# A state-space mixer's chunks in another column order, and sixteen small matmuls in another place

## The chip, the core and the metric

The kernel runs on one core of a Trainium2 chip. The metric is the device time of one execution in microseconds. PE is the matmul engine (PEld its weight loads), ACT the scalar engine, DVE the vector engine, POOL the general-purpose engine, SP the engine that issues most DMAs. Each engine executes its own list of instructions strictly in order; semaphores make one engine wait for another.

## What is computed

A transformer-like block on 512 tokens of width 1024, in fp32: a norm, an input projection, then two mixers side by side (a state-space mixer and a dilated attention), gates and an output projection, a feed-forward part with a three-tap convolution, a last gated branch and a norm. The change lies in the state-space mixer and beside the projections for the attention:

```python
z = rms_norm(x) @ w_in            # s_in (512), q, k, v (768 each), gates (2048)
# state-space mixer, 32 groups of 16 channels, 64 complex states per group
bu = einsum('blgh,gph->blgp', s_in, bbar)        # complex
s[l] = a * s[l-1] + bu[l]                        # along the sequence
y = gelu(einsum(s, c) + d * s_in); y = y * sigmoid(y @ glu_w + glu_b)
# attention: rotary on q and k, 12 heads of 64, three dilation patterns
```

## The kernel before

**Tokens and tiles.** Token 4c + r is held at column (or partition) c of residue r; r runs over 4, c over the 128 chunks of four tokens. "By residue" means tiles of 128 tokens with the same r, "by tile" means 128 tokens that follow each other (32 chunks with all four residues).

**Products.** Each fp32 weight chunk of 128 x 1024 is loaded by SP into wr (L127), copied by ACT to a high part wh (L128), and the rest is formed by DVE as the low part wl (L129). Each of the three rings has three buffers. One product is three matmuls of 512 columns (`mm3`, L149 to L151): high-high, high-low, low-high. PE's stream is thus almost wholly such triples, and each chunk of weights needs its ACT and its DVE step in time. `proj_tok` (L307) makes one 512-column projection of all tokens, one PSUM tile (pa) per residue; its evacuation runs ahead of other work in priority.

**Background work.** The state-space mixer is a Python generator, `g_ssm` (L424). After every second chunk `tick` (L275) lets it issue steps until a budget is used up; each `yield` names the cost that its author put down for the step. A scheduler turns the program order and the priorities (`ahead`) into one list of instructions per engine when the program is built, by its own estimate of times; nothing is reordered when it runs.

**The recurrence.** U holds the input by chunk (a transpose by PE, an evacuation by ACT, L656 to L660). es (L667) are the contributions of each chunk to the state, one set for the real and one for the imaginary part (i), for 16 pairs of groups (q). ACT writes them shifted by one chunk into E (L668), 128 columns per q. DVE then runs the recurrence over the chunks in steps of `cstep` (L680): four products into scr (the real and imaginary part, each times two factors), one sum into both parts, and two sums into one part each, all at L413, the line of the helper `tt`. The steps are, in order:

- three long steps over 32 columns per q, within blocks of four chunks (L695);
- three middle steps over 8 columns (L698), seven short steps over one column (L701), three middle steps over 7 columns (L704), on the last column of each block;
- three long steps over 31 columns (L707), which hand the block's start on to its other columns.

With 16 q, a long product has 512 (or 496) columns, and the sum into both parts 1024 (or 992). In the kernel before, chunk c stands in column c, so the long steps touch every fourth column and the middle steps every sixteenth. After them, ys (L717 to L719) takes E, U and two factor tensors to the outputs Yg, and yT (L725 to L729) is their transpose, evacuated by ACT.

**The projections for the attention.** After the state-space input come v (heads 4 to 11), then three projections j = 0, 1, 2 of q and k heads. ACT evacuates each residue (L372), DVE applies the rotary factors (L381 to L386, six operations of 64 columns), and PE transposes the result (`to_heads`, L392). These transposes are put on a list, `later`, and issued at the next tick. In PE's list they stand between matmuls of the next projection; the ones of j = 2 stand in the first v product.

**The factors by tile.** The norm's factor y1[0] is held by residue. L852 to L858 turn it into y1[1], by tile: sixteen matmuls of one column each into the PSUM tile yps, and one DVE copy, y1t (L857). Only the evacuation of the last v heads (L365) reads it. `ax_tile` tiles (yps, es, transposes and so on) share three PSUM buffers; a buffer is free again when the tile's last reader has finished.

Of the kernel before, what the change touches and what calls it, by code (L numbers as in the profile page):

```python
# [12 lines left out]
AF = mybir.ActivationFunctionType  # L13
# [8 lines left out]
R = 4  # L22
# [15 lines left out]
A_BUDGET = 3.4  # L38
# [26 lines left out]
def tile_hybrid_block(ctx: ExitStack, tc: tile.TileContext, xT, xtok, pT, W, vecs, consts, ssm, out):  # L65
    nc = tc.nc
    ACT, DVE, POOL, PE = nc.scalar, nc.vector, nc.gpsimd, nc.tensor
# [8 lines left out]
    def slot(i, shape, name, dt=F32):  # L76
        return sb.tile([P] + shape, dt, tag=f"s{i}", name=name)
# [4 lines left out]
    def mm_tile(name):  # L82
        return pm.tile([P, 512], F32, tag="mm", name=name)
# [4 lines left out]
    def t_tile(name):  # L88
        return ring.tile([P, 512], F32, tag="t", name=name, bufs=4)
# [19 lines left out]
    def ahead(offset=AHEAD):  # L109
        return tc.high_priority(offset=offset)  # L110
# [47 lines left out]
    def u_split(u, k, src, gcol, c=slice(0, SEQ)):  # L158
        ACT.activation(u[0][k][:, c], src[:, c], AF.Copy, scale=v1(gcol + k))  # L159
        DVE.scalar_tensor_tensor(u[1][k][:, c], src[:, c], v1(gcol + k), u[0][k][:, c].bitcast(F32), op0=ALU.mult, op1=ALU.subtract)  # L160
# [140 lines left out]
    def residue(a, r):  # L301
        return a[:, r * 128:(r + 1) * 128]
# [4 lines left out]
    def proj_tok(evac, first=False, budget=0.0, hooks=None):  # L307
        wA = WTiles(512)
        pss = [mm_tile(f"pa{r}") for r in range(R)]
        for k in range(KD):  # L310
            if first:
                with ahead():
                    if k:
                        u_split(u, k, x[:, k, :], V_MIX)
            w = wA.next()
            for r in range(R):
                mm3(pss[r], (residue(u[0][k], r), residue(u[1][k], r)), w, k == 0, k == KD - 1)
            if hooks and k in hooks:
                hooks[k]()
            if k % 2 == 1 and k < KD - 1:  # L320
                tick(budget)
        if first:

            with ahead(2 * AHEAD):
                for r in range(R):
                    evac(r, pss[r])
            tick(budget)
            return
        tick(budget)
        with ahead(2 * AHEAD):  # L330
            for r in range(R):
                evac(r, pss[r])
# [36 lines left out]
    def ev_qk(j):  # L369
        def ev(r, ps):  # L370
            t = t_tile("qk")
            ACT.activation(t, ps, AF.Copy, scale=y1[0][:, r:r + 1])  # L372
            th = t.rearrange("p (n d) -> p n d", d=64)
            x1 = th[:, :, 0:8]
            x2 = th[:, :, 8:16]
            cosb = rope[:, r, 0:1, :].to_broadcast([P, 8, 8])
            nsin = rope[:, r, 1:2, :].to_broadcast([P, 8, 8])
            psin = rope[:, r, 2:3, :].to_broadcast([P, 8, 8])
            a = ring.tile([P, 2, 8, 8], F32, tag="ra", name="ra", bufs=2)
            b = ring.tile([P, 2, 8, 8], F32, tag="rb", name="rb", bufs=2)  # L380
            DVE.tensor_tensor(a[:, 0], x1, cosb, op=ALU.mult)  # L381
            DVE.tensor_tensor(a[:, 1], x2, cosb, op=ALU.mult)
            DVE.tensor_tensor(b[:, 0], x2, nsin, op=ALU.mult)
            DVE.tensor_tensor(b[:, 1], x1, psin, op=ALU.mult)
            DVE.tensor_tensor(x1, a[:, 0], b[:, 0], op=ALU.add)
            DVE.tensor_tensor(x2, a[:, 1], b[:, 1], op=ALU.add)  # L386
            later.append(functools.partial(to_heads, r, t))

        def to_heads(r, t):
            pt = ax_tile("qkT")  # L390
            for i in range(4):
                PE.transpose(pt[:, i * 128:(i + 1) * 128], t[:, i * 128:(i + 1) * 128], ident)  # L392
            ptv = pt.rearrange("p (i n) -> p i n", i=4)
            n0 = 0
            if j == 0:

                n0 = 2
                ACT.activation(qk[0][:, 0:2, :].rearrange("p i (t r n) -> p i t r n", t=4, r=R)[:, :, :, r, :],
                               ptv[:, 0:2].rearrange("p i (t n) -> p i t n", t=4), AF.Copy)
            ACT.activation(qk[j][:, n0:4, r * 128:(r + 1) * 128], ptv[:, n0:4], AF.Copy)  # L400
        return ev
# [22 lines left out]
    def g_ssm():  # L424
# [133 lines left out]
        AA = {1: A[1], 2: A[2], 3: A[3], 4: A[4], 8: A8, 12: A12, 16: A16}  # L558
# [53 lines left out]
        for i in range(2):  # L612
            for q4 in range(4):
                ps = ax_tile("g1t")
# [39 lines left out]
        U = slot("U", [NQ, P], "U")  # L654
        for q4 in range(4):
            ps = ax_tile("ut")  # L656
            for q in range(4):
                PE.transpose(ps[:, q * 128:(q + 1) * 128], flat(S, q4 * 4 + q), ident)
            ACT.activation(U[:, q4 * 4:q4 * 4 + 4, :].rearrange("p q c -> p (q c)"), ps, AF.Copy)
            yield 0.15  # L660
        E = slot("x", [2, NQ, P], "E")
        DVE.memset(E[:, :, :, 0:1], 0.0)
        for i in range(2):
            for q4 in range(4):
                ps = ax_tile("es")
                for q in range(4):
                    PE.matmul(ps[:, q * 128:(q + 1) * 128], G1[i][:, q4 * 4 + q, :], U[:, q4 * 4 + q, :], start=True, stop=True)  # L667
                ACT.activation(E[:, i, q4 * 4:q4 * 4 + 4, 1:128], ps.rearrange("p (q c) -> p q c", q=4)[:, :, 0:127], AF.Copy)  # L668
                yield 0.15

        G2 = [slot(f"g{i}", [NQ, 2, R, H], f"G2{i}") for i in range(2)]
# [8 lines left out]
        def cstep(dst, src, a_, n):  # L680

            tv = scr[:, 0:2 * NQ * n].rearrange("p (i q n) -> p i q n", i=2, q=NQ)
            uv = scr[:, 1024:1024 + 2 * NQ * n].rearrange("p (i q n) -> p i q n", i=2, q=NQ)
            arb = a_[0].unsqueeze(2).to_broadcast([P, NQ, n])
            aib = a_[1].unsqueeze(2).to_broadcast([P, NQ, n])
            for i in range(2):
                tt(tv[:, i], src[:, i], arb, ALU.mult)
                tt(uv[:, i], src[:, i], aib, ALU.mult)
            tt(dst, dst, tv, ALU.add)
            tt(dst[:, 0], dst[:, 0], uv[:, 1], ALU.subtract)  # L690
            tt(dst[:, 1], dst[:, 1], uv[:, 0], ALU.add)

        E4 = E.rearrange("p i q (b f) -> p i q b f", f=4)
        E16 = E.rearrange("p i q (s f) -> p i q s f", f=16)
        for i in range(1, 4):  # L695
            cstep(E4[:, :, :, :, i], E4[:, :, :, :, i - 1], AA[1], 32)
            yield 4.77
        for i in range(1, 4):  # L698
            cstep(E16[:, :, :, :, 4 * i + 3], E16[:, :, :, :, 4 * i - 1], AA[4], 8)
            yield 1.53  # L700
        for s in range(1, 8):  # L701
            cstep(E16[:, :, :, s:s + 1, 15], E16[:, :, :, s - 1:s, 15], AA[16], 1)
            yield 0.58
        for i in range(3):  # L704
            cstep(E16[:, :, :, 1:8, 4 * i + 3], E16[:, :, :, 0:7, 15], AA[4 * (i + 1)], 7)
            yield 1.40
        for i in range(3):  # L707
            cstep(E4[:, :, :, 1:32, i], E4[:, :, :, 0:31, 3], AA[i + 1], 31)
            yield 4.64

        Yg = slot("S", [R, 32, H], "Yg")
        for q4 in range(4):
            ps = ax_tile("ys")
            for q in range(4):
                qq = q4 * 4 + q
                o = ps[:, q * 128:(q + 1) * 128]
                PE.matmul(o, U[:, qq, :], flat(T, qq), start=True, stop=False)  # L717
                PE.matmul(o, E[:, 0, qq, :], flat(G2[0], qq), start=False, stop=False)
                PE.matmul(o, E[:, 1, qq, :], flat(G2[1], qq), start=False, stop=True)  # L719
            ACT.activation(  # L720
# [3 lines left out]
        yT = slot("U", [4, SEQ], "yT")  # L724
        for mt in range(4):  # L725
            ps = ax_tile("yt")
            for r in range(R):
                PE.transpose(ps[:, r * 128:(r + 1) * 128], Yg[:, r, mt * 8:(mt + 1) * 8, :].rearrange("p g h -> p (g h)"), ident)
            ACT.activation(yT[:, mt, :], ps, AF.Copy)  # L729
            yield 0.15  # L730
        env["yT"] = yT

# [113 lines left out]
    hooks[R] = factors  # L846
    proj_tok(ev_v12, False, A_BUDGET, hooks)
    rb1 = rstd_bc(y1[0], "n1")
    for j in range(3):
        proj_tok(ev_qk(j), False, A_BUDGET)  # L850

    yps = ax_tile("yps")  # L852
    for t_ in range(4):
# [2 lines left out]
    yt_ = small([4], "y1t")  # L856
    DVE.tensor_copy(yt_, yps[:, 0:4])  # L857
    y1.append(yt_)  # L858
    for m in range(2):
        ps = mm_tile("v0")  # L860
        gemm(ps, KD, u)
        tick(A_BUDGET)
        with ahead():
            ev_v0(m, ps)
# [4 lines left out]
    for m in range(16):  # L869
        ps = mm_tile("gps")  # L870
        gemm(ps, KD, u)
        g = gt[m // 4][:, m % 4, :]
# [5 lines left out]
    yT, bh, bl = env["yT"], env["bh"], env["bl"]  # L878
# [16 lines left out]
    for m in range(4):  # L895
        ps = mm_tile("lps")
# [36 lines left out]
    for m in range(KD):  # L933
        ps = mm_tile("ops")
# [10 lines left out]
    for part in range(2):  # L945
# [28 lines left out]
        for m in range(KD):  # L974
            ps = mm_tile("dps")
# [13 lines left out]
    for m in range(KD):  # L989
        ps = mm_tile("pps")  # L990
# [31 lines left out]
    for m in range(KD - NLAST):  # L1022
        ps = mm_tile("eps")
# [25 lines left out]
    for gi, rs in enumerate(LAST):  # L1049
        c = slice(rs[0] * 128, rs[-1] * 128 + 128)  # L1050
        end = gi == len(LAST) - 1
        for m in tail:
            ps = mm_tile("eps")[:, 0:128 * len(rs)]
# [174 lines left out]
```

## Time and profile before

| | us |
|---|---|
| median of 3 runs | 820.05 (820.04 to 821.41) |
| the profiled execution, its own time | 820.38 |
| its span, first to last instruction | 818.3 |
| PE busy | 801.2 (98%) |
| DVE busy | 508.5 (62%) |
| ACT busy | 346.4 (42%) |
| mean granted TensorE clock | 0.987 |

The span is what the profile's views cover; about 2.1 us lie around it. A busy PE says that it had work, not at which clock. Matmuls overlap, so that rows of 0.39 us follow each other every 0.23 us at the full clock; rows of DVE and ACT overlap by about 0.1 us as well. In the views below, times are in microseconds from the start of the span, except means, which are marked or given in ns.

### The profile page before, as it was taken

Reading aid. Unit: us, or ns where it says so; the run is one execution under the profiler, and the core shown is the slowest. Engines: PE = TensorE matmul, PEld = TensorE weight load, DVE = VectorE, ACT = ScalarE, POOL = GpSimd, SP = SyncE. Lnnn points to the kernel's source line nnn. Section 1 sums busy time; section 2 is a strip of 40 time slices with the busy share of each in tenths; the row PEclk is TensorE's granted clock in tenths of the full one; section 3 lists DMA queues with packets and bytes.
Section 4 is the critical chain, followed back from the end, with each engine's and each line's share of the span. In section 5 each row is a group of like instructions: output and inputs, shape, how many; then the busy total and the mean of one; then the engine's idle time right before and its main releaser. Section 6 shows DMA issues by size and latency. Waiting matters only on the chain.

```text
span 818.3 us, 10848 instructions
## 1 busy us (share of the span) xinstructions
PE 801.2 (98%) x4294; PEld 664.3 (81%) x4294; DVE 508.5 (62%) x944; ACT 346.4 (42%) x543; POOL 10.9 (1%) x10
## 2 busy tenths in 40 slices
PE   9999989799999999999999999999999999999996
PEld 7888868589777788888888888888888888888886
DVE  7963999992354447855776555332565556445586
ACT  6773632335344434344354433222344434335454
POOL 2001000000000000000000000000000000000000
PEclk9999998799999999999999999999999999999999
DMA  7731111122111123442322233223322332233202
GB/s 279 269 99 57 51 53 59 70 82 74 53 52 53 53 78 103 139 153 96 128 98 85 101 103 104 88 92 104 103 94 88 104 103 87 95 103 103 81 23 103
DMA packets 23810, 78.97 MB, mean 97 GB/s; under 512 B 2640, under 2 KB 3024, under 8 KB 23760
## 3 DMA queue, kind: packets, MB, share of 16 engines
q1 hardware_dynamic: 23616, 78.22, 28.2%
q8 instruction: 33, 0.54, 0.3%
q14 instruction: 17, 0.14, 0.1%
q10 hardware_dynamic: 144, 0.07, 0.0%
HBM read 76.18 MB, written 2.10 MB: 96 GB/s over the span
## 4 chain that ended last, share of the span: by engine, by line
PE 86%; DVE 10%; ACT 2%; issue 1%; DMA 0%; DVEq 0%; ACTq 0%
PE pg L151 5%; PE pu L151 5%; PE dps L150 5%; PE dps L151 5%; PE pu L150 5%; PE pu L149 5%; PE pg L150 5%; PE pg L149 5%; PE dps L149 5%; PE gps L149 4%; PE gps L151 4%; PE gps L150 4%; DVE E L413 3%; DVE scr L413 2%; PE pa L150 2%; PE pa L151 2%
## 5 line engine op out<-in xcount | busy, mean ns | idle before, releaser
L128 ACT ACTIVATE wh<-wr 128x1024 fp32r<-128x1024 f32 (+1 forms) x132 | 138.1, 1047 | 297.7 <-issue 61.6
L129 DVE TENSOR_TENSOR wl<-wr,wh 128x1024 fp32r<-128x1024 f32 (+1 forms) x132 | 160.0, 1213 | 68.2 <-ACT wh L128 67.9
L150 PE MATMUL pu<-u2l,wh 128*128 128x512 f32 x176 | 68.5, 389 | 0.0
L149 PE MATMUL pu<-u2h,wh 128*128 128x512 f32 x176 | 68.5, 389 | 0.0
L151 PE MATMUL pg<-u2h,wl 128*128 128x512 f32 x176 | 68.5, 389 | 0.0
L149 PE MATMUL pg<-u2h,wh 128*128 128x512 f32 x176 | 68.5, 389 | 0.0
L150 PE MATMUL pg<-u2l,wh 128*128 128x512 f32 x176 | 68.5, 389 | 0.0
L149 PE MATMUL dps<-ah,wh 128*128 128x512 f32 x176 | 68.5, 389 | 0.0
L150 PE MATMUL dps<-al,wh 128*128 128x512 f32 x176 | 68.5, 389 | 0.0
L151 PE MATMUL dps<-ah,wl 128*128 128x512 f32 x176 | 68.5, 389 | 0.0
L151 PE MATMUL pu<-u2h,wl 128*128 128x512 f32 x176 | 68.5, 389 | 0.0
L150 PE MATMUL pa<-wl,u1h 128*128 128x512 f32 x160 | 63.3, 396 | 0.4 <-DVE u1l L160 0.4
L149 PE MATMUL pa<-wh,u1h 128*128 128x512 f32 x160 | 63.5, 399 | 0.2 <-ACT u1h L159 0.2
L151 PE MATMUL pa<-wh,u1l 128*128 128x512 f32 x160 | 62.7, 394 | 0.0
L149 PE MATMUL gps<-u1h,wh 128*128 128x512 f32 x128 | 51.3, 401 | 0.0
L151 PE MATMUL gps<-u1h,wl 128*128 128x512 f32 x128 | 50.5, 394 | 0.0
L150 PE MATMUL gps<-u1l,wh 128*128 128x512 f32 x128 | 50.2, 392 | 0.0
L413 DVE TENSOR_TENSOR ext<-pg,n_y 128x512 f32<-128x512 f32 x22 | 15.2, 692 | 44.1 <-PE pg L151 44.1
L413 DVE TENSOR_TENSOR gt<-gps,n_bc 128x512 f32<-128x512 f32 x16 | 11.1, 693 | 47.0 <-PE gps L151 47.0
L150 PEld LDWEIGHTS pu<-u2l,wh 128*128 128x128 f32 x176 | 33.0, 188 | 6.9
L150 PEld LDWEIGHTS pg<-u2l,wh 128*128 128x128 f32 x176 | 33.0, 188 | 6.9
L149 PEld LDWEIGHTS dps<-ah,wh 128*128 128x128 f32 x176 | 33.0, 188 | 6.9
(304 smaller groups left out, 1566.1 us busy)
## 6 DMA issues: line engine op xcount, KB each, us to landing
wr<-in_W_dram SPq DMA_DIRECT2D x128, 512.0 KB, 3.2
xt<-in_xtok_dram SPq DMA_DIRECT2D x4, 512.0 KB, 7.9
h<-in_xT_dram SPq DMA_DIRECT2D x8, 256.0 KB, 4.9
out_dram<-fo SPq DMA_DIRECT2D x8, 256.0 KB, 2.3
x<-in_xT_dram SPq DMA_DIRECT2D x7, 256.0 KB, 5.6
wr<-in_W_dram SPq DMA_DIRECT2D x4, 256.0 KB, 5.5
cst<-in_consts_dram SPq DMA_DIRECT2D x1, 568.0 KB, 10.3
sp<-in_ssm_dram SPq DMA_DIRECT2D x1, 544.0 KB, 7.3
```

Of the source, the lines that this page charges most:

```text
L128: ACT.activation(hi[:, c], raw[:, c], AF.Copy)
L129: DVE.tensor_tensor(lo[:, c], raw[:, c], hi[:, c].bitcast(F32), op=ALU.subtract)
L149: PE.matmul(ps, st[0], mv[0], start=first, stop=False)
L150: PE.matmul(ps, st[0], mv[1], start=False, stop=False)
L151: PE.matmul(ps, st[1], mv[0], start=False, stop=last)
L413: DVE.tensor_tensor(o, a, b, op=op)
```

## The change

Chunks are kept in another column order. Chunk c = 4b + f stands in column 32f + b in U and in E. U's evacuation reads its PSUM tile permuted, so that the matmuls es come out in the new order. The shift by one chunk is now two evacuations: blocks f = 1 to 3 take columns 0 to 95, and block 0 takes columns 96 to 126. The long steps touch 32 (or 31) adjacent columns per q, the middle steps every fourth column. yT's evacuation reads its PSUM tile permuted, which gives back the old order. The costs named by the yields are the same, as are the number of the DVE operations and their columns.

Apart from that, the three QK projections are issued after the products for the factors by tile instead of before them.

```diff
-            ACT.activation(U[:, q4 * 4:q4 * 4 + 4, :].rearrange("p q c -> p (q c)"), ps, AF.Copy)
+            ACT.activation(U[:, q4 * 4:q4 * 4 + 4, :].rearrange("p q (i b) -> p q i b", i=4),
+                           ps.rearrange("p (q b i) -> p q i b", q=4, i=4), AF.Copy)
...
         E = slot("x", [2, NQ, P], "E")
+        E4 = E.rearrange("p i q (f b) -> p i q b f", f=4)
+        E16 = E.rearrange("p i q (f s g) -> p i q s g f", f=4, g=4)
...
-                ACT.activation(E[:, i, q4 * 4:q4 * 4 + 4, 1:128], ps.rearrange("p (q c) -> p q c", q=4)[:, :, 0:127], AF.Copy)
+                psq = ps.rearrange("p (q c) -> p q c", q=4)
+                ACT.activation(E[:, i, q4 * 4:q4 * 4 + 4, 32:128], psq[:, :, 0:96], AF.Copy)
+                ACT.activation(E[:, i, q4 * 4:q4 * 4 + 4, 1:32], psq[:, :, 96:127], AF.Copy)
...
-        E4 = E.rearrange("p i q (b f) -> p i q b f", f=4)
-        E16 = E.rearrange("p i q (s f) -> p i q s f", f=16)
         for i in range(1, 4):
             cstep(E4[:, :, :, :, i], E4[:, :, :, :, i - 1], AA[1], 32)
             yield 4.77
         for i in range(1, 4):
-            cstep(E16[:, :, :, :, 4 * i + 3], E16[:, :, :, :, 4 * i - 1], AA[4], 8)
+            cstep(E16[:, :, :, :, i, 3], E16[:, :, :, :, i - 1, 3], AA[4], 8)
             yield 1.53
         for s in range(1, 8):
-            cstep(E16[:, :, :, s:s + 1, 15], E16[:, :, :, s - 1:s, 15], AA[16], 1)
+            cstep(E16[:, :, :, s:s + 1, 3, 3], E16[:, :, :, s - 1:s, 3, 3], AA[16], 1)
             yield 0.58
         for i in range(3):
-            cstep(E16[:, :, :, 1:8, 4 * i + 3], E16[:, :, :, 0:7, 15], AA[4 * (i + 1)], 7)
+            cstep(E16[:, :, :, 1:8, i, 3], E16[:, :, :, 0:7, 3, 3], AA[4 * (i + 1)], 7)
             yield 1.40
         for i in range(3):
             cstep(E4[:, :, :, 1:32, i], E4[:, :, :, 0:31, 3], AA[i + 1], 31)
...
-            ACT.activation(yT[:, mt, :], ps, AF.Copy)
+            ACT.activation(yT[:, mt, :].rearrange("p (r b i) -> p r b i", r=R, i=4),
+                           ps.rearrange("p (r i b) -> p r b i", r=R, i=4), AF.Copy)
...
     rb1 = rstd_bc(y1[0], "n1")
-    for j in range(3):
-        proj_tok(ev_qk(j), False, A_BUDGET)

     yps = ax_tile("yps")
...
     y1.append(yt_)
+    for j in range(3):
+        proj_tok(ev_qk(j), False, A_BUDGET)
     for m in range(2):
```

## Rows read from the trace of the kernel before

**Rows 1.** The page's part 1: busy time, share of the span and instructions.

```profile
PE 801.2 (98%) x4294; PEld 664.3 (81%) x4294; DVE 508.5 (62%) x944; ACT 346.4 (42%) x543; POOL 10.9 (1%) x10
```

**Rows 2.** Busy time by stretch; columns as the first line says.

```profile
core 0: us, PE busy (x) PEld busy (x) DVE busy (x) ACT busy (x) POOL busy (x), PEclk, DMA share, GB/s
...
120.00:130.00 10.00, 7.18 (x28) 6.20 (x29) 9.93 (x40) 3.09 (x5) 0.00 (x0) 0.66 0.31 105
...
150.00:160.00 10.00, 4.61 (x18) 3.78 (x19) 9.93 (x31) 2.84 (x5) 0.00 (x0) 0.61 0.31 105
160.00:170.00 10.00, 10.00 (x45) 8.32 (x44) 9.97 (x10) 4.29 (x11) 0.00 (x0) 0.87 0.17 54
```

**Rows 3.** PE's waits: who for whom, us in total, times, longest.

```profile
PE qkT L392 <- DVE qk L386: 7.1, 2, 3.9
PE qkT L392 <- DVE y1t L857: 1.7, 1, 1.7
```

**Rows 4.** PE in time at the first stall: start, length, what, [idle before <-releaser].

```profile
122.82 2.79 PE L392 MATMUL qkT<-cst,qk 128*128 128x128 f32 x12 [3.22 <-DVE qk L386]
...
128.40 0.40 PE L151 MATMUL pa<-wh,u1l 128*128 128x512 f32 x1
```

**Rows 5.** PE in time at the second stall.

```profile
153.69 1.94 PE L392 MATMUL qkT<-cst,qk 128*128 128x128 f32 x8 [3.90 <-DVE qk L386]
157.33 1.09 PE L392 MATMUL qkT<-cst,qk 128*128 128x128 f32 x4 [1.69 <-DVE y1t L857]
...
162.48 0.42 PE L149 MATMUL v<-u1h,wh 128*128 128x512 f32 x1
```

**Rows 6.** DVE in time over one long step ahead of the first stall.

```profile
112.45 4.00 DVE L413 TENSOR_TENSOR scr<-E,apw 128x512 f32<-128x512 f32 x4
...
116.35 2.04 DVE L413 TENSOR_TENSOR E<-E,scr 128x1024 f32<-128x1024 f32 x1
...
118.22 1.29 DVE L129 TENSOR_TENSOR wl<-wr,wh 128x1024 fp32r<-128x1024 f32 x1
...
119.35 2.11 DVE L413 TENSOR_TENSOR E<-E,scr 128x512 f32<-128x512 f32 x2
```

**Rows 7.** DVE's groups by form: count, busy us, mean ns, idle before.

```profile
L413 DVE TENSOR_TENSOR scr<-E,apw 128x512 f32<-128x512 f32 x12 | 12.2, 1075 | 4.3 <-ACT E L668 4.3
...
L413 DVE TENSOR_TENSOR E<-E,scr 128x1024 f32<-128x1024 f32 x3 | 6.1, 2020 | 0.0
...
L413 DVE TENSOR_TENSOR ex<-sp,apw 128x1024 f32<-128x1024 f32 x4 | 4.8, 1220 | 0.8 <-PE es L667 0.8
...
L413 DVE TENSOR_TENSOR scr<-E,pv 128x128 f32<-128x128 f32 x12 | 3.9, 367 | 0.0
...
L413 DVE TENSOR_TENSOR E<-E,scr 128x256 f32<-128x256 f32 x3 | 1.8, 611 | 0.0
...
L413 DVE TENSOR_TENSOR yl<-yT,yh 128x512 fp32r<-128x512 f32 x4 | 2.7, 685 | 0.2 <-ACT yh L882 0.2
```

**Rows 8.** DVE in time at the second stall.

```profile
149.66 2.94 DVE L413 TENSOR_TENSOR scr<-E,apw 128x496 f32<-128x496 f32 x3
...
153.32 0.23 DVE L386 TENSOR_TENSOR qk<-ra,rb 128x64 f32<-128x64 f32 x1
...
156.76 0.23 DVE L386 TENSOR_TENSOR qk<-ra,rb 128x64 f32<-128x64 f32 x1
157.02 0.16 DVE L857 COPY y1t<-yps 128x4 f32<-128x4 f32 x1
```

**Rows 9.** ACT: one row in time, then groups by form.

```profile
112.16 2.73 ACT L372 ACTIVATE qk<-pa,n_y 128x512 f32<-128x512 f32 x4 [2.29 <-PE pa L151]
...
L668 ACT ACTIVATE E<-es 128x508 f32<-128x508 f32 x8 | 4.8, 595 | 2.4 <-PE es L667 2.4
...
L365 ACT ACTIVATE V<-vT,y1t 128x128 f32<-128x128 f32 x8 | 2.3, 369 | 2.9 <-DVE E L413 2.2 <-PE vT L363 0.7
...
L659 ACT ACTIVATE U<-ut 128x512 f32<-128x512 f32 x4 | 2.0, 595 | 0.0
```

**Rows 10.** DVE in time where it waits for a weight's high part.

```profile
57.82 1.22 DVE L129 TENSOR_TENSOR wl<-wr,wh 128x1024 fp32r<-128x1024 f32 x1 [3.73 <-ACT wh L128]
```

## The prediction

> **What bounds the kernel now.** I read the page's engine line first [rows 1]: PE is busy for 801.2 of 818.3 us, so nothing that only shortens DVE or ACT work moves the time unless it removes a stretch in which PE stands still or runs slowly. The second view, the stretches of ten microseconds, finds those stretches [rows 2]: from 120 to 130 PE is busy 7.18 of 10 at a mean granted clock of 0.66, from 150 to 160 it is busy 4.61 at 0.61, and the next ten are full but at 0.87. DVE is busy for 9.93, 9.93 and 9.97 of those same three stretches. The third view, PE's waits, names the cause [rows 3]: the transposes of L392 waited 7.1 us in two places for the rotary operations of L386 on DVE, and once 1.7 us for the copy y1t of L857, also on DVE.
>
> PE's own order in time gives the size. First stall: PE waits 3.22 us until 122.82, then runs at the lower of its two levels (1.2 GHz) until the matmuls are back at 0.40 us at 128.40 [rows 4]. At half rate 5.58 us hold 2.8 us of work, so 2.8 us are lost on top. Second stall: 3.90 us until 153.69, 1.69 us until 157.33, and the lower level until 162.48 [rows 5]; the 8.79 us less the 1.69 us of waiting are 7.1 us at half rate, 3.55 lost. Sum: 3.22 + 2.8 + 3.90 + 1.69 + 3.55 = 15.2 us. That is all this change can return here: outside of it PE is fed.
>
> Why DVE is late: it works through the long steps of the recurrence, in order, and the rotary operations stand behind them. One long step is four products (112.45 to 116.35), the 1024-column sum (to 118.22), a weight split wl (to 119.35) and two 512-column sums, which end at 121.46 [rows 6]; the first rotary result follows and frees PE at 122.82.
>
> **The change, part by part.** *Long steps over adjacent columns.* Today the operands of these steps step by four columns. A product of 512 columns takes 1075 ns and a sum of 1024 takes 2020 ns [rows 7]. The rows for dense operands are an ex product, also with a broadcast factor, 1220 ns for 1024, and yl, two dense operands, 685 ns for 512 [rows 7]. So neither the broadcast nor adding in place is what costs; the stride is. Rows of DVE overlap by about 0.1 us (the four products fill 3.90, not 4.30), so I take 0.60 for 512 and 1.13 for 1024. A step was 3.90 + 1.87 + 2.0 (2.11 less the overlap) = 7.77 us without wl, and becomes 4 x 0.60 + 1.13 + 2 x 0.60 = 4.73: 3.0 saved. Bounds: no overlap at all (0.69 and 1.22) leaves 2.4 per step; no gain at all is a rival below. The three last steps have 31 columns and a destination that begins one column later; only their four first products stand ahead of the second stall, three of them filling 2.84 us, 0.95 each [rows 8].
>
> Lead of DVE at the first rotary work: three steps, but two of the first step's products run before DVE waits 0.8 us for es on ex [rows 7], and that wait swallows their 0.75. So 2.25 + 3.0 + 3.0 = 8.25 us, and a first rotary result at 122.7 becomes one at 114.4. That wants the four evacuations of L372, which run from 112.16 to 114.89 [rows 9], 0.68 apart; the rotary work of one residue takes 0.8 (at the second stall three more results follow in 3.44 us with one wl of 1.13 between [rows 8]), so the last comes by about 116.7. PE reaches its transposes at 122.82 - 3.22 = 119.60. The first stall goes with about 3 us to spare, and the clock has no reason to fall there: 6.0 us.
>
> At the second stall PE now arrives at 149.79 - 6.0 = 143.8. DVE has 8.25 plus four products at 0.95 - 0.58 = 0.37, in all 9.75 us of lead, so the first rotary result, 153.55 [rows 8], comes at 143.8: a draw. The next two residues come 0.8 apart, while four transposes, 1.09 us at the lower level [rows 5], take PE about 0.5: 0.3 of waiting each. The fourth stands behind a wl and ends at 156.99 - 9.75 = 147.2, some 0.6 after PE arrives. About 1.2 us of waiting is left; I take 2, since a draw is more easily lost than won. With waits this short and broken I expect the clock to stay up.
>
> *The products of the factors by tile (yps, y1t).* Sixteen tiny matmuls and one DVE copy of 0.16 us [rows 8] move from behind the three QK projections to just behind rb1; no DMA is among them. On PE they pass all three projections and need only y1[0], which rb1's own matmuls already wait for, so they add no wait. On DVE the copy is issued ahead of all of the recurrence, near a place where DVE stands idle 3.73 us for a weight [rows 10]; if that cover were gone it would hold up wl by 0.16. It holds one of the three auxiliary PSUM buffers until the copy. What it frees: today the third set of transposes needs the buffer that y1t empties only at 157.18; that 1.69 us goes, and next late there is the rotary work counted above.
>
> *U and yT through a strided PSUM read.* Eight ACT evacuations of 512 columns, 595 ns each for U [rows 9], now read every fourth (U) or thirty-second (yT) column. No ACT row of before reads PSUM that way. From below: unchanged, as the write side is dense. From above: the ratio of DVE's strided to dense row, 1075 to 685, or 1.6. At U the chain transpose, evacuate, es is exposed on PE, about twice the extra; at yT once: at 1.6, 0.36 x 3 = 1.1 us. I take 0.6. By the Trainium skill, Advanced Engine Details and Errata, PSUM Cachelines, every two consecutive fp32 values should be adjacent for best throughput, which speaks against these reads; it states no price for ACT, and no row of before shows one.
>
> *E in two evacuations.* 508 columns at 595 ns become 384 and 124; a 128-column evacuation takes 369 [rows 9], so the pair needs about 0.87. Eight times 0.27 is 2.2 us of ACT. They hide behind es, whose groups of matmuls leave ACT idle 2.4 us over the eight [rows 9]. If that cover is gone, es waits for its buffer, up to 2 us. I take 0, keeping 1 for the range.
>
> *Middle steps.* Their columns step by 4 in place of 16. At a step of 16 a sum of 256 takes 611 ns, at a step of 4 one of 512 products takes 1075 [rows 7]: 2.1 to 2.4 ns a column with the fixed part, so no difference is taken. The three of eight columns hold 3.9 us of products, 1.8 of sums of 256 [rows 7] and about as much of sums of 128, the three of seven a little less: some 14 us of DVE ahead of the second stall. A tenth either way is 1.4 us.
>
> Sum against the profiled execution of 820.38 us (span 818.3 and 2.1 around it): 15.2 - 2 (left at the second stall) - 0.6 = 12.6 us, so 807.8; the median of the runs is 0.33 lower, so 807.5. I say 808.
>
> **The rivals.** *All of it returns*: DVE wins the draw and the reads are free. 820.05 - 15.2 = 804.9. For it: rows that overlap well. Against: rotary work of 0.8 us a residue paces the transposes anyway.
>
> *The second stall stays.* DVE is 2 us or more late at 143.8, PE waits long enough for the clock to fall again [rows 2], and only the first stall and y1t's wait come back: 6.0 + 1.7 less a little, 813. It decides from about 2 us of DVE time: dense steps at 0.69 and 1.22 would cost it (3 x 0.6), or middle steps a sixth slower (2.3 us). A rule of the Trainium skill speaks for it: Vector Engine (DVE) Microarchitecture Reference, Measured stream behaviour on trn2, says that a port hopping every element pays more for small steps than for large ones. Rows of before disagree: 4 columns cost no more than 16 [rows 7].
>
> *The rate does not change*, because something else than the stride sets it: the time stays at 819 to 821. The ex and yl rows speak against.
>
> *Slower: ACT's strided reads.* The exposed extra is three times that of one evacuation, so from a read that takes 4.2 us more, eight times 0.595, the gain of 12.6 is eaten; at ten times the time would be 823. DVE's ratio of 1.6 speaks against, but no ACT row excludes it. The same end comes if the order that the planner finds for the moved matmuls puts rotary work behind further long steps: each 1.1 us.
>
> **How the numbers follow.** Forecast (806 to 811) 0.58; all of it 0.10; second stall stays (811 to 815) 0.21; unchanged 0.05; slower 0.06. Leaving out unchanged and slower and a little at either end, 804.6 to 814.5 holds 8 in 10. A measurement of this kernel tells about 0.2%, 1.6 us, from no change: faster 0.89, same 0.05, slower 0.06.
>
> **What would show it.** After: products of 512 columns near 0.69 us and sums of 1024 near 1.22; the first wait of L392 gone and a clock of 1.00 from 110 to 140; y1t early and no wait on it; the second wait under 2 us in all and no lower clock around 145. Evacuations of U and yT at 0.6 to 0.95. I am wrong if the long steps keep their durations, if L392 still waits over 2 us with a clock below 1.00, or if ACT's U rows pass 1.5 us and PE waits at es.

## The result, and the profile after

| | before | after |
|---|---|---|
| median of the runs, us | 820.04 (819.55 to 821.41) | 808.34 (807.97 to 809.45) |
| profiled execution, us | 820.38 | 807.97 |
| its span, us | 818.3 | 806.2 |

The ratio after to before is 0.9857 (95% interval 0.984 to 0.9874): 11.7 us faster by the medians, 12.4 us between the two profiled executions. One run of e4 below took 2057.46 us, where its ten others lie between 819.91 and 821.82, and is left out of its range and ratio.

The page's part 1 of after. PE is busy 5.4 us less than in [rows 1] with the same number of instructions, because fewer of its matmuls ran at the lower clock; DVE is busy 18.7 us less, also with the same number; ACT has eight more instructions for the same time in all:

```profile
PE 795.8 (99%) x4294; PEld 659.8 (82%) x4294; DVE 489.8 (61%) x944; ACT 346.3 (43%) x551; POOL 10.9 (1%) x10
```

Busy time by stretch, after (columns as the first line says), to be laid beside [rows 2]:

```profile
core 0: us, PE busy (x) PEld busy (x) DVE busy (x) ACT busy (x) POOL busy (x), PEclk, DMA share, GB/s
...
120.00:130.00 10.00, 9.91 (x52) 8.18 (x52) 9.77 (x45) 4.07 (x6) 0.00 (x0) 1.00 0.29 103
...
140.00:150.00 10.00, 8.38 (x46) 6.37 (x45) 9.97 (x34) 4.27 (x8) 0.00 (x0) 1.00 0.26 79
150.00:160.00 10.00, 10.00 (x48) 8.12 (x47) 9.96 (x15) 3.83 (x10) 0.00 (x0) 1.00 0.23 81
160.00:170.00 10.00, 10.00 (x46) 8.29 (x45) 6.14 (x8) 4.74 (x5) 0.00 (x0) 1.00 0.40 134
```

The first hole, 7.18 busy of 10 at a clock of 0.66, is closed; of the second a dent is left, 8.38 of 10, and the clock stays at 1.00 through it. DVE is as full as before until 160, but from there on it now has time to spare (6.14).

PE's waits from 85 to 185 us, after (engine, line, for whom: us, times, longest). One line stands where [rows 3] had two:

```profile
PE qkT L392 <- DVE qk L386: 1.6, 4, 0.8
```

PE in time, after, at the places of [rows 4] and [rows 5]. The first twelve transposes now follow the matmul before them without a wait; at the second place four short waits are left (in brackets):

```profile
120.06 0.39 PE L151 MATMUL pa<-wh,u1l 128*128 128x512 f32 x1
120.29 1.47 PE L392 MATMUL qkT<-cst,qk 128*128 128x128 f32 x12
...
123.51 0.39 PE L151 MATMUL pa<-wh,u1l 128*128 128x512 f32 x1
...
143.94 0.39 PE L151 MATMUL v<-u1h,wl 128*128 128x512 f32 x1
145.09 0.63 PE L392 MATMUL qkT<-cst,qk 128*128 128x128 f32 x4 [0.76 <-DVE qk L386]
145.90 0.63 PE L392 MATMUL qkT<-cst,qk 128*128 128x128 f32 x4 [0.19 <-DVE qk L386]
146.71 0.63 PE L392 MATMUL qkT<-cst,qk 128*128 128x128 f32 x4 [0.18 <-DVE qk L386]
...
148.52 0.52 PE L392 MATMUL qkT<-cst,qk 128*128 128x128 f32 x3 [0.48 <-DVE qk L386]
...
154.23 0.39 PE L149 MATMUL gps<-u1h,wh 128*128 128x512 f32 x1
```

DVE in time, after: one long step as in [rows 6], then the first and the last rotary result of the first place, the first and the last of the second (as in [rows 8]), and the sums that follow it:

```profile
107.95 2.49 DVE L413 TENSOR_TENSOR scr<-E,apw 128x512 f32<-128x512 f32 x4
110.36 1.22 DVE L413 TENSOR_TENSOR E<-E,scr 128x1024 f32<-128x1024 f32 x1
111.50 1.22 DVE L129 TENSOR_TENSOR wl<-wr,wh 128x1024 fp32r<-128x1024 f32 x1
112.63 1.29 DVE L413 TENSOR_TENSOR E<-E,scr 128x512 f32<-128x512 f32 x2
...
114.94 0.22 DVE L386 TENSOR_TENSOR qk<-ra,rb 128x64 f32<-128x64 f32 x1
...
117.51 0.23 DVE L386 TENSOR_TENSOR qk<-ra,rb 128x64 f32<-128x64 f32 x1
...
144.72 0.22 DVE L386 TENSOR_TENSOR qk<-ra,rb 128x64 f32<-128x64 f32 x1
...
148.15 0.22 DVE L386 TENSOR_TENSOR qk<-ra,rb 128x64 f32<-128x64 f32 x1
148.29 2.49 DVE L413 TENSOR_TENSOR E<-E,scr 128x992 f32<-128x992 f32 x3
```

Groups by form, after (count, busy us, mean ns of one, idle before), first DVE's, which answer to [rows 7], then ACT's, which answer to [rows 9]:

```profile
L413 DVE TENSOR_TENSOR scr<-E,apw 128x512 f32<-128x512 f32 x12 | 7.6, 686 | 4.3 <-ACT E L674 4.3
...
L413 DVE TENSOR_TENSOR scr<-E,pv 128x128 f32<-128x128 f32 x12 | 4.0, 376 | 0.0
...
L413 DVE TENSOR_TENSOR E<-E,scr 128x1024 f32<-128x1024 f32 x3 | 3.7, 1218 | 0.0
L413 DVE TENSOR_TENSOR E<-E,scr 128x992 f32<-128x992 f32 x3 | 3.6, 1186 | 0.0
...
L413 DVE TENSOR_TENSOR E<-E,scr 128x256 f32<-128x256 f32 x3 | 1.9, 632 | 0.0
```

```profile
L673 ACT ACTIVATE E<-es 128x384 f32<-128x384 f32 x8 | 3.9, 490 | 1.9 <-PE es L671 1.9
...
L674 ACT ACTIVATE E<-es 128x124 f32<-128x124 f32 x8 | 2.2, 269 | 0.0
...
L733 ACT ACTIVATE yT<-yt 128x512 f32<-128x512 f32 x4 | 2.1, 612 | 0.0
L660 ACT ACTIVATE U<-ut 128x512 f32<-128x512 f32 x4 | 2.0, 594 | 0.0
```

**Where the 12.4 us went.** The same matmuls can be taken by their start times in both traces. For that, three more rows of PE in time, of before:

```profile
119.21 0.39 PE L151 MATMUL pa<-wh,u1l 128*128 128x512 f32 x1
...
149.41 0.39 PE L151 MATMUL v<-u1h,wl 128*128 128x512 f32 x1
...
166.62 0.39 PE L149 MATMUL gps<-u1h,wh 128*128 128x512 f32 x1
```

From the last matmul ahead of the first transposes to the one that is back at full rate: 119.21 to 128.40 [rows 4] before, 120.06 to 123.51 after; 9.19 against 3.45, so 5.74 came back. From the last v matmul ahead of the second transposes to the first gate matmul (gps): 149.41 to 166.62 before, 143.94 to 154.23 after; 17.21 against 10.29, so 6.92. The matmuls of yps take about 0.5 from one place and give it to another. The kernel's first stretch, which the change does not touch, ended 0.3 later in this execution. 5.74 + 6.92 - 0.3 = 12.4: the two stalls are all of it. The spans differ by only 12.1, since the last norm took 0.25 longer in this execution; what lies around the span makes up for that.

### The profile page after: what moved, and what is told of

Its sections match the earlier page's. It is cut to its first block, busy times and chain, and to the rows that moved or that the text cites. A ratio compares the mean times of both kernels' runs of the same rounds, so it can differ in the third digit from the quotient of the medians.

```text
span 806.2 us, 10860 instructions
## 1 busy us (share of the span) xinstructions
PE 795.8 (99%) x4294; PEld 659.8 (82%) x4294; DVE 489.8 (61%) x944; ACT 346.3 (43%) x551; POOL 10.9 (1%) x10
## 4 chain that ended last, share of the span: by engine, by line
PE 86%; DVE 9%; ACT 2%; issue 1%; DMA 1%; SPq 0%; DVEq 0%; ACTq 0%
PE pu L151 5%; PE dps L151 5%; PE pg L151 5%; PE dps L150 5%; PE pu L149 5%; PE pu L150 5%; PE pg L149 5%; PE pg L150 5%; PE dps L149 5%; PE gps L149 4%; PE gps L151 4%; PE gps L150 4%; PE pa L151 2%; PE pa L150 2%; DVE E L413 2%; PE pa L149 2%
## 5 line engine op out<-in xcount | busy, mean ns | idle before, releaser
L413 DVE TENSOR_TENSOR ext<-pg,n_y 128x512 f32<-128x512 f32 x22 | 15.2, 692 | 44.1 <-PE pg L151 44.1
L150 PEld LDWEIGHTS dps<-al,wh 128*128 128x128 f32 x176 | 33.0, 188 | 6.9
```

What stands on the lines that cost most here:

```text
L150: PE.matmul(ps, st[0], mv[1], start=False, stop=False)
L413: DVE.tensor_tensor(o, a, b, op=op)
```

## The experiments

The theory: the long steps' rate makes DVE late, and PE's two stalls are that lateness. Rivals for the cause: the moved products of the factors (y1t), or the order of the work alone, without the rate. The first four runs were made on one chip, where before had 820.25; the next four on another, where it had 820.27. Before, e1 and e3 have the same list of operations in the same order on PE, and the same on DVE; so have e2 and after. All ratios are to before on the same chip, with 95% intervals.

**The new order, the products of the factors left where they were** (run e1_order_only, an edit of after):

```
     rb1 = rstd_bc(y1[0], "n1")
 
+    for j in range(3):
+        proj_tok(ev_qk(j), False, A_BUDGET)
     yps = ax_tile("yps")
...
     y1.append(yt_)
-    for j in range(3):
-        proj_tok(ev_qk(j), False, A_BUDGET)
```

> The column order alone; the products of the factors by tile stay behind the three QK projections. Theory (the column order carries nearly all of the gain, and y1t's copy is one more wait at the second stall): DVE reaches y1t only after the last rotary work, so the third set of transposes waits some 1.7 us again; 810 us if the lower clock stays away. Rival (that wait, added to the 1.6 us that the changed kernel still has there, is long enough to bring the lower clock back): 812 to 813. Second rival (y1t was a cost of its own in no way): 808.3.

Measured: 811.38 us (810.06 to 812.42), 0.9889 (0.9875 to 0.9902). The waits ahead of the first two sets of transposes shrink to 0.17 and 0.19, but the third set of transposes waits for the buffer that y1t empties, and the mean clock of the ten microseconds behind it falls to 0.83. The four runs come in two pairs, 810.06 and 810.53 near the theory, 812.23 and 812.42 on the rival; the one profiled is the slowest. PE in time, and the stretch:

```profile
149.52 0.63 PE L392 MATMUL qkT<-cst,qk 128*128 128x128 f32 x4 [2.19 <-DVE y1t L862]
```

```profile
150.00:160.00 10.00, 10.00 (x46) 8.32 (x44) 9.93 (x16) 3.77 (x8) 0.00 (x0) 0.83 0.30 103
```

So the new order brings most of the gain, and moving y1t is worth some 2 to 3 us on top of it by this run: 811.38 against 808.34 and 809.39 in the two measurements of after, which were made beside other runs of before.

**The products of the factors moved, all else as before** (run e2_factors_only, an edit of before):

```
     rb1 = rstd_bc(y1[0], "n1")
-    for j in range(3):
-        proj_tok(ev_qk(j), False, A_BUDGET)
 
     yps = ax_tile("yps")
...
     y1.append(yt_)
+    for j in range(3):
+        proj_tok(ev_qk(j), False, A_BUDGET)
```

> The kernel before with the products of the factors by tile moved, columns as before. Theory (DVE, not y1t, sets when PE gets on; PE's wait of 1.69 us only moves to the next thing that DVE delivers, a weight's low part after 175 us): 819 to 820.2, with a new wait of PE on wl. Rival (the wait is worth itself wherever it stands): 818.3.

Measured: 819.69 us (819.32 to 822.94), ratio 1.0 (0.9989 to 1.001): nothing that can be told, as the theory said. The wait for y1t is gone, and its time stands in other waits. PE in time: the second wait for rotary work, 3.90 in [rows 5], is 5.74, and further on PE waits for a weight split that DVE has not yet reached:

```profile
154.69 2.79 PE L392 MATMUL qkT<-cst,qk 128*128 128x128 f32 x12 [5.74 <-DVE qk L386]
...
177.80 0.75 PE L151 MATMUL gps<-u1h,wl 128*128 128x512 f32 x1 [1.97 <-DVE wl L129]
```

The lower clock even lasted less long at the two stalls (means of 0.83, 0.83 and 1.00 from 120 to 130, 150 to 160 and 160 to 170, where [rows 2] has 0.66, 0.61 and 0.87; behind the new wait 0.89 and 0.94 from 170 to 190), and it brought nothing: with DVE setting the pace, a PE that runs faster between two waits waits longer at the second. The same move is worth nothing that can be told without the dense steps and 1 to 3 us with them (e1 here and e3 below); the parts of this change do not add. Since DVE and PE have after's lists here, in after's order, the order of the work alone gives none of the gain.

**The dense steps alone** (run e3_dense_steps_only, an edit of before: the two views of E alone, so that the recurrence pairs other columns than the reference's; evacuations and y1t as before, and every engine's instructions in the same order as before):

```
-        E4 = E.rearrange("p i q (b f) -> p i q b f", f=4)
-        E16 = E.rearrange("p i q (s f) -> p i q s f", f=16)
+        E4 = E.rearrange("p i q (f b) -> p i q b f", f=4)
+        E16 = E.rearrange("p i q (f s g) -> p i q s g f", f=4, g=4)
...
-            cstep(E16[:, :, :, :, 4 * i + 3], E16[:, :, :, :, 4 * i - 1], AA[4], 8)
+            cstep(E16[:, :, :, :, i, 3], E16[:, :, :, :, i - 1, 3], AA[4], 8)
...
```

> The kernel before; only the views through which the recurrence addresses its columns are the new ones, so that the long steps are dense. U, E and yT are filled and read in the old order: the recurrence runs over wrongly paired columns. No ACT instruction and no place of yps differs from before. Theory (the rate of DVE's long steps is the whole cause; the permuted and split evacuations cost nothing): the same as the column order alone within 0.5 us, about 810. Rival (the permuted evacuations and the split cost PE time): faster than the column order alone by 0.6 to 2 us. Second rival (something else of the change, not the rate, gives the gain): 820.

Measured: 810.28 us (808.49 to 811.24), 0.9875 (0.9859 to 0.9892). One group by form (a sum of 1024 takes 1219 ns), and PE in time:

```profile
L413 DVE TENSOR_TENSOR scr<-E,apw 128x512 f32<-128x512 f32 x12 | 7.6, 685 | 4.3 <-ACT E L668 4.3
```

```profile
148.13 1.09 PE L392 MATMUL qkT<-cst,qk 128*128 128x128 f32 x4 [2.19 <-DVE y1t L857]
```

The steps have after's rate, the remaining wait is e1's, and so is the time, within the intervals. Between this run and e1 lie only the strided reads of U and yT and E's split evacuations. The medians alone do not settle what these cost: 1.1 us lie between them, which is in the rival's range, and the intervals overlap. PE's starts settle it. First e1, then e3, from U's transposes to es:

```profile
77.08 1.47 PE L658 MATMUL ut<-cst,S 128*128 128x128 f32 x12
...
79.36 7.41 PE L671 MATMUL es<-U,G 128*128 128x128 f32 x64
```

```profile
75.72 1.47 PE L658 MATMUL ut<-cst,S 128*128 128x128 f32 x12
...
78.02 7.40 PE L667 MATMUL es<-U,G 128*128 128x128 f32 x64
```

From the first transpose to the end of es PE takes 9.7 us in both, and from the first ys to the last transpose for yT 17.9 in both (174.80 to 192.69, 173.08 to 190.97). What differs between the two executions is the stretch before, which ended 1.36 later in e1 (77.08 against 75.72), and 0.4 between es and ys, most of it in the matmuls behind the long wait, part of which ran at the lower level. So these evacuations cost PE nothing. By the rows, yT takes 610 ns here and U 595 in [rows 9], and 612 and 594 with strided reads in after.

**Everything of after, but the six long steps strided** (run e4_all_strided, an edit of after; these steps pair other columns than the reference's):

```
         E4 = E.rearrange("p i q (f b) -> p i q b f", f=4)
+        E4s = E.rearrange("p i q (b f) -> p i q b f", f=4)
...
-            cstep(E4[:, :, :, :, i], E4[:, :, :, :, i - 1], AA[1], 32)
+            cstep(E4s[:, :, :, :, i], E4s[:, :, :, :, i - 1], AA[1], 32)
...
-            cstep(E4[:, :, :, 1:32, i], E4[:, :, :, 0:31, 3], AA[i + 1], 31)
+            cstep(E4s[:, :, :, 1:32, i], E4s[:, :, :, 0:31, 3], AA[i + 1], 31)
```

> The changed kernel with all of its edits, but the six long steps address every fourth column as before, so that the recurrence runs over wrongly paired columns. Theory: both stalls and the lower clock are back, 819 to 820.5, as with the factors moved alone. Rival (the new places of instructions help by themselves): under 818.

Measured: 820.71 us (819.91 to 821.82), ratio 1.0001 (0.9992 to 1.0009), with a product of 512 columns at 1061 ns and a sum of 1024 at 2005 ns, and both stalls back. One group by form, and PE in time:

```profile
L413 DVE TENSOR_TENSOR scr<-E,apw 128x512 f32<-128x512 f32 x12 | 12.2, 1061 | 4.3 <-ACT E L675 4.3
```

```profile
123.81 2.75 PE L392 MATMUL qkT<-cst,qk 128*128 128x128 f32 x12 [3.21 <-DVE qk L386]
...
156.31 2.89 PE L392 MATMUL qkT<-cst,qk 128*128 128x128 f32 x12 [7.00 <-DVE qk L386]
```

With e3 this settles the cause from both sides: with the rate alone nearly all of the gain is there, with all else and without the rate none of it. DVE's order is not quite after's in this run (see e6, which has the same); e2, with after's order and the strided rate, says the same.

**Three of the six strided.** Is it DVE's time that counts, or where it is saved? Three steps before the middle ones and three behind them cost DVE nearly the same: strided, its busy time in the page's part 1 is 9.9 and 8.6 us above after's. The first three strided (run e5_first_three_strided, an edit of after):

```
+        E4s = E.rearrange("p i q (b f) -> p i q b f", f=4)
...
-            cstep(E4[:, :, :, :, i], E4[:, :, :, :, i - 1], AA[1], 32)
+            cstep(E4s[:, :, :, :, i], E4s[:, :, :, :, i - 1], AA[1], 32)
```

> The changed kernel; the first three long steps address every fourth column again (wrongly paired columns), the last three stay dense. Theory (the lead of DVE at the transposes counts; the first three steps give 8.25 of the 9.75 us): the first stall is back whole, over 3 us and the lower clock, and the second too, some 3 to 4 us; 816.5 to 818. Rival (DVE time counts alike wherever it is saved, three of six steps for half of the gain): 814.

The last three strided (run e6_last_three_strided, an edit of after):

```
+        E4s = E.rearrange("p i q (b f) -> p i q b f", f=4)
...
-            cstep(E4[:, :, :, 1:32, i], E4[:, :, :, 0:31, 3], AA[i + 1], 31)
+            cstep(E4s[:, :, :, 1:32, i], E4s[:, :, :, 0:31, 3], AA[i + 1], 31)
```

> The changed kernel; the last three long steps address every fourth column again (wrongly paired columns). Theory: the first stall stays away; at the second, the four products ahead of it take 1.5 us more, so the first wait there grows from 0.8 to about 2.2 and the clock may fall; behind it DVE has some 7 us more to do and PE gets a new wait on a weight's low part near 167 us; 811 to 812.5. Rival (what stands behind the transposes is hidden): 809.8. Second rival (DVE time counts alike wherever it is saved): 814.

Measured: e5 818.05 us (817.18 to 818.97), 0.9973 (0.9961 to 0.9984); e6 812.73 us (811.91 to 813.61), 0.9906 (0.9892 to 0.9919). Both lie a little above what the theory said (816.5 to 818 and 811 to 812.5), as after on this chip lies 1.1 above its 808.3, and away from the rivals. Against 809.39 for after on that chip the first three are worth 8.7 us and the last three 3.3, which includes a move that the next paragraphs show. PE in time, first e5, where both stalls are back, then e6, where only the second is:

```profile
124.88 0.63 PE L392 MATMUL qkT<-cst,qk 128*128 128x128 f32 x4 [3.15 <-DVE qk L386]
...
154.60 2.79 PE L392 MATMUL qkT<-cst,qk 128*128 128x128 f32 x12 [3.62 <-DVE qk L386]
```

```profile
147.87 2.89 PE L392 MATMUL qkT<-cst,qk 128*128 128x128 f32 x12 [3.60 <-DVE qk L386]
```

Most of what the last three steps save lies behind the rotary work for which PE waits, and nobody waits for it soon: in e6 DVE stays full to 170 with PE busy 9.99 of 10 from 160 on, and a new wait for a weight split there, which I had thought likely, did not come.

The 3.3 us are not the price of the stride alone. DVE's list in e5 is after's, but in e6 (and e4) the scheduler put some operations elsewhere. The one that counts is the first sum of 992 columns: in after it follows the last rotary result of the second place (148.29), in e6 it stands ahead of the first. DVE in time, e6:

```profile
145.53 1.92 DVE L413 TENSOR_TENSOR E<-E,scr 128x992 f32<-128x992 f32 x1
...
147.49 0.23 DVE L386 TENSOR_TENSOR qk<-ra,rb 128x64 f32<-128x64 f32 x1
```

It holds that result up by 1.83 us (the next operation starts at 147.36), so of the wait of 3.60 only some 1.8 would be left without it. Whether the lower level would then have followed, no run shows.

**After, once more** (run after_again, no edit):

> The changed kernel itself, beside the others on the same chip: 808.3.

Measured: 809.39 us (808.55 to 810.03), 0.9864 (0.9851 to 0.9878), with the same 1.6 us of waits.

**After, without the waits that it has left** (run e7_late_heads, an edit of after: the last projection's transposes, and the evacuations of both v products, put behind both products, so that PE has the second product's matmuls, 5 us of them, to run before it needs the rotary work):

```
-    def tick(budget):
-        while later:
+    def tick(budget, heads=True):
+        while heads and later:
...
+    vps = []
     for m in range(2):
-        ps = mm_tile("v0")
-        gemm(ps, KD, u)
-        tick(A_BUDGET)
-        with ahead():
-            ev_v0(m, ps)
+        vps.append(mm_tile("v0"))
+        gemm(vps[m], KD, u)
+        tick(A_BUDGET, m == 1)
+    with ahead():
+        for m in range(2):
+            ev_v0(m, vps[m])
```

> The changed kernel, with the last QK projection's transposes and the two evacuations of v put behind both v products in place of the first. Theory (the 1.6 us that PE still waits for rotary work are all that DVE still costs PE): PE has 24 more matmuls, 5.4 us, ahead of the transposes, the four waits go, 806.7. Rival (the work only moves: PSUM buffers of the v products or the later start of the attention bring a new wait): 808 to 810.

Measured: 806.72 us (805.42 to 807.39), 0.983 (0.9816 to 0.9845): faster than both kernels, 2.7 us below after on the same chip, though after's waits are only 1.6. PE in time, and the stretch:

```profile
149.24 0.39 PE L151 MATMUL v<-u1h,wl 128*128 128x512 f32 x1
149.47 1.47 PE L392 MATMUL qkT<-cst,qk 128*128 128x128 f32 x12
150.70 0.48 PE L149 MATMUL gps<-u1h,wh 128*128 128x512 f32 x1
```

```profile
140.00:150.00 10.00, 10.00 (x48) 8.31 (x47) 9.97 (x35) 2.05 (x3) 0.00 (x0) 1.00 0.27 87
```

The waits are longer than the profile counts them. It counts from the end of a matmul, but in an unbroken row the next one starts before that end: matmuls of 0.39 stand 0.23 apart, and the twelve transposes here fill 1.23 us (149.47 to 150.70), 0.41 for four, where four in front of a wait in after fill 0.62 (145.09 to 145.90, less the 0.19). So each wait hides 0.16 to 0.21 more, and after's four are 1.6 + 0.7 = 2.3 us. The starts say the same: from the first v matmul to the first chunk product (ys) after takes 32.4 us (138.7 to 171.1), e7 30.2 (138.6 to 168.8), so 2.2 were left, with the same matmuls between in both. The other 0.5 us of the 2.7 is within what executions differ by: the first 76 us of after, which after_again, e4, e5, e6 and e7 run in the same order, end anywhere from 76.0 to 77.6. So the hit on 806.7 is in part luck: the theory took 1.6 off 808.3, where 2.7 came off 809.39.

## Why the prediction was right, step by step

808.0 was forecast, 808.34 measured, and by the forecast's own mechanism. Its steps:

**The rate.** 685 and 1220 ns were forecast from the dense rows [rows 7]; 686 and 1218 came, without a difference for the broadcast factor or the sum in place. The long step, forecast at 4.73, fills 2.41 (107.95 to 110.36) + 1.14 + 1.21 (112.63 to the next operation at 113.84) = 4.76.

**The lead of DVE.** Forecast 8.25 us at the first rotary result and 9.75 at the second. The recurrence's input starts 0.87 later in after's execution (first es matmul 77.75 before, 78.62 after), so the results are to be moved by that. First: 122.7 became 115.16, 7.5 earlier, 8.4 with the 0.87 (and the wait for es on ex grew from 0.8 to 1.6, as counted). Second: 153.55 became 144.94, 8.6 earlier, 9.5 with it. The last of the first four came at 117.74 against "about 116.7" (117.6 with the shift), and PE reached it at 120.29: 2.6 us to spare where "about 3" was said.

**The draw at the second place.** DVE was to give its first result when PE came, the fourth 0.6 after PE; 1.2 us of waits were counted and 2 taken. Measured: 0.76 + 0.19 + 0.18 + 0.48 = 1.61, of which 0.76 is the draw lost, and 2.2 with the overlap of matmuls that each wait breaks (e7). The value taken was right; that a wait costs 0.2 more than its length was not among its reasons.

**The clock.** It was said to stay up with waits "this short and broken", and it did. e1 and e3 show how near the other way was: one wait of 2.19 there was followed by the lower level, and the second rival (813, chance 0.21) is about what e6 with its 3.60 became, 812.73.

**The returnable 15.2 us.** The two stalls gave 5.74 and 6.92; with the 2.2 left that is 14.9, so the account of waits and half rate held within 0.3. That it did is partly chance: the matmuls of the first stall lost 2.4 to the lower clock, not 2.8 (the 5.58 us of them before take 3.22 in after, 120.29 to 123.51), and the three waits cost about 0.5 more than their lengths (e7).

**The products of the factors.** It was to add no wait and to free 1.69: after shows no wait on y1t, its copy stands at 53.01, and the matmuls of yps cost PE about 0.5 at either place. But 1.69 was no size of its own. Without the dense steps it is 0 within 0.9 us (e2), with them 1 to 3 us (e1 and e3 against the two measurements of after), since the wait grows to 2.19 and the lower clock follows it. The sum was saved from this because it counted both stalls as one account, with what is left at the end subtracted.

**The strided reads.** This term was mis-sized: 0.6 taken (0 to 1.1), 0 measured. U takes 594 ns against 595 [rows 9], and yT 612 against 610 dense (e3), and PE's starts around them are the same (e1 beside e3). The lower bound was right. DVE's ratio, from which the upper end came, says nothing of ACT. The rule of the Trainium skill weighed there (Advanced Engine Details and Errata, PSUM Cachelines: every two consecutive elements adjacent for best throughput) is not seen in these reads, which step by 4 and by 32 fp32 values.

**E in two evacuations.** 490 + 269 = 759 ns for a pair where 0.87 was said; the es matmuls from first to last take the same time, 7.13 us, in both traces (77.75 to 84.88, 78.62 to 85.75), so it costs nothing, as taken.

**The middle steps.** "No difference" was within 4%: a product of 128 takes 376 ns at a step of 4 against 367 at 16, a sum of 256 632 against 611 [rows 7]. Here the Trainium skill's page (Vector Engine (DVE) Microarchitecture Reference, Measured stream behaviour on trn2) has the sign, small steps dearer than large ones; by the rows of all these steps together it is a fiftieth, where the rival that it spoke for wanted a sixth.

**The sum.** Forecast 15.2 - 2 - 0.6 = 12.6; between the profiled executions 14.9 - 2.2 - 0 - 0.3 = 12.4. A cost that did not come (0.6) offset three small ones: 0.3 in the account of the stalls, 0.2 at the second place, 0.3 in the first stretch, which is chance.

## What to carry to other kernels

When an engine off the bottleneck is late for it, count its lead in microseconds at each place where the bottleneck meets it, not its total time: three steps made faster ahead of the meeting were worth 8.7 us here, three nearly equal ones mostly behind it about 3.3, a part of which is the moved sum of e6. Before such a lead is there, removing a single wait in front of the bottleneck can be worth nothing, as in e2, since the next wait on the same engine takes it over. When one run is to tell what a rate is worth, compare the lists of operations first: in e6 the scheduler had moved one across the meeting. Where a short wait is left once the lead is used up, look for other matmuls to put in front of it before making the late engine faster still.

## What was not expected of the hardware

- ACT reads PSUM at a step of 4 or of 32 fp32 values at the rate of adjacent ones: 594 and 612 ns for 512 columns (U and yT of after), beside 595 (U of before) and 610 (yT of e3).
- DVE's price for a step of 4 fp32 values is 1.57 times for a product of 512, where one source has the step (1075 ns beside 686), and 1.66 for a sum of 1024, where a source and the destination have it (2020 beside 1218); a run of 31 columns whose destination starts one column later has the dense rate (a sum of 992 in 1186 ns, beside 1218 for 1024).
- A wait that breaks a row of matmuls costs 0.16 to 0.21 us more than the profile shows, because matmuls in a row overlap (four transposes fill 0.62 us ahead of a wait, 0.41 in a row of twelve).
- Waits of 0.76, 0.19, 0.18 and 0.48 between 144.3 and 148.5 left the granted clock at 1.00; one of 2.19 (e1, e3) or 3.60 (e6) was followed by the lower level (means of 0.83 in e1, 0.87 in e3 and 0.86 in e6 over ten microseconds).
